# A two-layer encoder trunk on one core: the query norm's VectorE chain queued behind the query transposes, and a reordered opening

## The chip, the core and the metric

The kernel runs on one core of a Trainium2 chip. The metric is the device time of one execution in microseconds (us). A profile records one execution: when each instruction ran on TensorE (PE, its weight loads PEld), VectorE (DVE), ScalarE (ACT), GpSimd (POOL) and on SyncE's queue (SP), and what released it when it had waited.

## The reference

An encoder of two layers on one sequence of 512 tokens, 1024 wide, in float32. What matters here is the first feed-forward block and the query path of the attention branch:

```python
def rms_norm(x, g):
    y = x * rsqrt(mean(x * x, axis=-1) + EPS)
    return y * g
def swiglu(h, w_in, w_out):
    a, b = split(h @ w_in, 2)
    return (silu(a) * b) @ w_out
for l in range(2):
    x = x + 0.5 * swiglu(rms_norm(x, ffn1_norm[l]), ffn1_w_in[l], ffn1_w_out[l])
    h = rms_norm(x, mix_norm[l])
    q, k, v, gu, gv, lx, ly, g = split(h @ w_mix_in[l])
    q = apply_axial_rope(rms_norm(q.reshape(b, s, 8, 64), q_norm[l]), tabs)
    k = apply_axial_rope(rms_norm(k.reshape(b, s, 2, 64), k_norm[l]), tabs)
    ...   # attention, gated MLP, bidirectional LRU; gated sum; output projection
    ...   # cross-attention into 256 memory tokens; a second swiglu block
return rms_norm(x, final_norm)
```

## The kernel before

Activations lie transposed: feature tiles of 128 on the partitions, the 512 tokens along the free dimension. `x` holds 8 such tiles (`KD` = 8). Every float32 operand of a large product is split into a high part (`whi`, `xh`: a cast on ScalarE) and a low part (`wlo`, `xl`: a subtraction on VectorE), and `mm3` issues three matmuls for each product: high by high, high by low, low by high (lines 357 to 359 of the profile).

Weights stream in one order fixed by `plan()`. `Stream.load` starts the DMA of a chunk into one of two `stage` buffers from SyncE's queue. `Stream.split` makes high and low part of a *part* (half a chunk, 1024 columns) in one of four `whi`/`wlo` buffers, up to three parts ahead of the matmuls that take it. The first chunk comes in four smaller parts (256, 256, 512 and 1024 columns), so that the first product can begin early.

A *unit* (`pair_unit`) is 48 matmuls of 512 columns into two PSUM banks; `wide_unit` does 96 into four. All PSUM tiles rotate through one pool of eight banks, so a unit waits until the tile eight places earlier has been read.

**The opening.** `Norm.parts(m)` makes `xh` and `xl` of tile m. `Norm.square(m)` squares the tile on ScalarE and adds it to `nacc` on GpSimd (line 429). After the first unit `norm.finish()` splits `nacc`, sums it over the partitions with two matmuls against `ones_r` (line 395, in `row_scale`), and makes the row `s_row` (lines 400 to 403), by which each unit's result is scaled (lines 533 to 536). SyncE issues the DMAs for `x`, for the small parameters `par` and for the weights in turn, one every 0.47 us.

**The mixer.** While TensorE works through the input projection, side tasks (`attention`, `lru`, `gmlp`: Python generators in `tasks`) are advanced by `tick()`, so their instructions are laid in between. A scheduler then orders each engine's queue by dependences and priorities; each engine works its queue strictly in that order. In `attention`, the query's head norm is `head_squares` (ScalarE squares, line 743, and VectorE reductions `cqq`, line 744), and `head_scale` (a chain of 14 small VectorE operations of 128x32 with the Newton steps of `rsqrt_small`, lines 754 to 760, and one more at line 822 which makes `cq8`). `cq8` is first read by the scores of the attention heads, which come only after the `gu` unit. The rotated queries are transposed on TensorE (line 807, four token tiles t = 0 to 3, a PSUM bank each), copied out on ScalarE (line 813) and split on VectorE (line 816). In the same stretch run a step of the LRU (lines 633 to 663: sigmoid, exponential, tanh, square root on ScalarE; scans on VectorE; its block-diagonal weights split at line 486) and the units `ly` (two, with gelu at line 959) and `gv` (a `wide_unit`).

**Names.** `lam_prep` is a chain of tiny VectorE operations (`lz`) on LRU parameters, once a layer.

Of the kernel before, what the change touches and what calls it, by code (L numbers as in the profile page):

```python
# [14 lines left out]
P = 128  # L15
# [4 lines left out]
L = 2  # L20
# [236 lines left out]
def emit(tc, wts, par, rows, ws_t, bd, xt, memt, const, out):  # L257
# [16 lines left out]
    eps_t = keep.tile([P, 1], F32, name="eps_t")  # L274
    warm = keep.tile([P, 1], F32, name="warm")
    mem_row = keep.tile([P, MEM], F32, name="mem_row")
    pr = [keep.tile([P, NPC], F32, name=f"par{l}") for l in range(L)]
    lam_c = [keep.tile([P, 8], F32, name=f"lam{l}") for l in range(L)]
    keep.tile([P, PAD], F32, name="pad")
    x = keep.tile([P, KD, S], F32, name="x")  # L280
# [5 lines left out]
    def getr(n):  # L286
        return arena.get(n, F32R)
# [77 lines left out]
    def tick(n=1):  # L365
        for _ in range(n):
            for t in list(tasks):
                try:
                    next(t)
                except StopIteration:  # L370
                    tasks.remove(t)
# [35 lines left out]
    class Norm:  # L407


        def __init__(self, gain):  # L410
            self.gain = gain

        def tile(self, m):
            self.parts(m)
# [7 lines left out]
        def square(self, m):  # L422
            if m == 0:
                self.acc = row_p.tile([P, 512], F32, tag="nacc", name="nacc")
                act.activation(self.acc, x[:, m], AF.Square)
                return
            sq = get(1)
            act.activation(sq.f, x[:, m], AF.Square)  # L428
            pool.tensor_tensor(self.acc, self.acc, sq.f, op=ALU.add)  # L429
            sq.free()  # L430

        def sums(self):
# [50 lines left out]

    def split_to(hi, lo, src):
        act.copy(hi, src)  # L485
        dve.tensor_tensor(lo, src, hi.bitcast(F32), op=ALU.subtract)  # L486

    def pair_unit(tag, l, c, bh, bl, n=512, mid=0):
        ps = [bank(), bank()]
        k = 0  # L490
        while k < KD:
            if k == KD // 2:
                tick(mid)
            hi, lo = ws.take((tag, l, c))
            hi = hi.rearrange("p (k t c) -> p k t c", t=2, c=P)
            lo = lo.rearrange("p (k t c) -> p k t c", t=2, c=P)
            for i in range(hi.shape[1]):
                for t in range(2):
                    mm3(ps[t][:, 0:n], hi[:, i, t], lo[:, i, t], bh[k], bl[k], k == 0, k == KD - 1)
                k += 1  # L500
        return ps
# [19 lines left out]


    def ffn(l, w_in, w_out, norm, nxt):
        s_row = None
        for b in range(NB):
            gs = []
            for j in range(b * JB, (b + 1) * JB):
                psa, psb = pair_unit(w_in, l, j, xhk, xlk)
                if s_row is None:
                    s_row = norm.finish()  # L530
                t = get(1)
                g = getr(2)
                dve.tensor_tensor(t.f, psa, s_row, op=ALU.mult)  # L533
                mark["silu"] = act.activation(t.f, t.f, AF.Silu).ins  # L534
                pool.tensor_tensor(t.f, t.f, s_row, op=ALU.mult)  # L535
                dve.tensor_tensor(t.f, t.f, psb, op=ALU.mult)  # L536
                split_to(g.r[:, 0:512], g.r[:, 512:1024], t.f)
                t.free()
                gs.append(g)
                tick()  # L540
            for m in range(KD):
                if b == NB - 1 and m == KD - 1 and isinstance(nxt, FinalNorm):
                    parts = [ws.take((w_out, l, b, m)) for _ in range(2)]
                    for h in range(2):
                        cs = slice(h * 256, h * 256 + 256)
                        ps = bank()[:, 0:256]
                        for k in range(JB):
                            hi, lo = parts[k // 6]
                            c = slice(k % 6 * P, (k % 6 + 1) * P)
                            mm3(ps, hi[:, c], lo[:, c], gs[k].r[:, 0:512][:, cs], gs[k].r[:, 512:1024][:, cs],  # L550
                                k == 0, k == JB - 1)
                        dve.scalar_tensor_tensor(x[:, m, cs], ps, 0.5, x[:, m, cs], op0=ALU.mult, op1=ALU.add)
                        nxt.half(h)
                    continue
                ps = bank()
                for h, (k0, k1) in enumerate(((0, 6), (6, 11))):
                    hi, lo = ws.take((w_out, l, b, m))
                    for k in range(k0, k1):
                        c = slice((k - k0) * P, (k - k0 + 1) * P)
                        mm3(ps, hi[:, c], lo[:, c], gs[k].r[:, 0:512], gs[k].r[:, 512:1024],  # L560
                            k == 0, k == JB - 1)
                dve.scalar_tensor_tensor(x[:, m], ps, 0.5, x[:, m], op0=ALU.mult, op1=ALU.add)
                if b == NB - 1:
                    nxt.tile(m)
                tick()
            for g in gs:
                g.free()


    def mixer(l, norm, nxt):  # L570
# [192 lines left out]
        def attention():  # L763
# [39 lines left out]
            for t in range(NTT):  # L803
                ps = bank()
                for pr_ in range(4):
                    c0 = t * 512 + pr_ * P
                    pe.transpose(ps[:, pr_ * P:(pr_ + 1) * P], qrot.f[:, c0:c0 + P], ident)
                p3 = ps.rearrange("p (a b) -> p a b", a=4)
                parts = []
                for e in range(2):  # L810
                    q4 = qt[e].r.rearrange("p (a b) -> p a b", a=4)[:, :, t * P:(t + 1) * P]
                    own = slice(e * 64, e * 64 + 64)
                    act.copy(q4[own], p3[own])
                    parts.append((q4, own, slice(64 - e * 64, 128 - e * 64)))
                for q4, own, oth in parts:
                    dve.tensor_tensor(q4[oth], p3[own], q4[own].bitcast(F32), op=ALU.subtract)
                if t == 1:
                    yield
            qrot.free()
            cq = head_scale(qss, 8, "cq")  # L820
            cq8 = small.tile([P, 8, NTT], F32, tag="cq8", name="cq8")
            dve.tensor_scalar(cq8, cq, HD ** -0.5, None, op0=ALU.mult)
            yield
# [422 lines left out]
    def lam_prep(l):  # L1246

        lam = pr[l][:, PC["lam"]:PC["lam"] + 8]
        z = [small.tile([P, 8], F32, tag=f"lz{i}", name=f"lz{i}") for i in range(5)]
        dve.tensor_scalar(z[0], lam, -1.0, None, op0=ALU.mult)  # L1250
        dve.tensor_tensor(z[1], lam, z[0], op=ALU.min)
        with tc.issue_after(mark["silu"]):
            act.activation(z[1], z[1], AF.Exp)
# [13 lines left out]
        return pr[l][:, PC[nm]:PC[nm] + 8]  # L1267

    def load_x(j):
        m0, m1 = ((0, 1), (1, 2), (2, 4), (4, 8))[j]  # L1270
        sp.dma_start(out=x[:, m0:m1], in_=xt[:, m0:m1])
        if j == 0:
            sp.dma_start(out=pr[0], in_=par[:, 0])

    pool.memset(ones, 1.0)
    pool.memset(eps_t, EPS)
    dve.tensor_copy(ones_r, ones)
    ws.load([(0, 256), (256, 512), (512, 1024), (1024, 2048)], load_x)
    nrm = Norm(gains(0, "ffn1"))
    ps = bank()  # L1280
    for _ in range(9):
        pe.matmul(ps[:, 0:P], lhsT=ones, rhs=ones, start=True, stop=True)
# [2 lines left out]
        for m in ms:  # L1285
            nrm.parts(m)
    ws.load()
    sp.dma_start(out=pr[1], in_=par[:, 1])
    sp.dma_start(out=cst, in_=const)
    for m in range(KD):  # L1290
        nrm.square(m)
# [31 lines left out]
```

## Time and profile before

| | us |
|---|---|
| median of three runs (2667.14 to 2667.82) | 2667.79 |
| the profiled execution, by the clock of the runs | 2665.21 |
| its span in the trace | 2663.4 |
| TensorE busy in the span | 2626.9 (99%) |
| VectorE, ScalarE, GpSimd busy | 1391.7, 1163.3, 399.4 |

The profiled execution lies 2.6 us below the median of the runs. A matmul's busy time overlaps the next one's: 512 columns show 0.39 us each, but follow one another every 0.227 us at the full clock. "Granted clock" is the share of TensorE's full clock (2.4 GHz) that the chip allowed; 0.50 is 1.2 GHz. What matters is where TensorE stood idle, and which engine's result ended each wait.

### The profile page before, as it was taken

How to read it: one execution, taken by the hardware profiler on the slowest of the kernel's cores; microseconds unless marked ns; L12 is line 12 of the kernel's file. 1: busy time of each engine (PE TensorE's matmuls, PEld its weight loads, DVE VectorE, ACT ScalarE, POOL GpSimd, SP SyncE). 2: the span in 40 equal slices, each digit the busy share in tenths (PEclk: the TensorE clock that was granted, in tenths of full speed). 3: DMA queues.
4: the chain of work that ended last, by engine and by line, in shares of the span. 5: the costliest groups of instructions: out<-in, count | busy, mean ns of one | idle time of the engine just before them, and what ended most of it. 6: DMA issues, size and time to landing. Idle time of an engine off the chain costs nothing.

```text
span 2663.4 us, 30204 instructions
## 1 busy us (share of the span) xinstructions
PE 2626.9 (99%) x12213; PEld 2187.6 (82%) x12213; DVE 1391.7 (52%) x1965; ACT 1163.3 (44%) x1656; POOL 399.4 (15%) x301
## 2 busy tenths in 40 slices
PE   9999999999999999999999999999999999999998
PEld 7888888788878888888888888878888888888886
DVE  6434457766655554334443344587675664643343
ACT  5322337966634443222332223488575343422223
POOL 3101115100021021001111011240000300210111
PEclk9999999999999999999999999999999999999999
DMA  5232232222223222232322322322222232322222
GB/s 181 80 118 103 77 115 72 87 72 71 95 103 112 91 99 103 80 111 87 111 95 84 128 95 76 120 77 71 72 80 98 93 127 80 111 86 97 109 77 75
DMA packets 50123, 254.31 MB, mean 95 GB/s; under 512 B 5440, under 2 KB 11072, under 8 KB 31808
## 3 DMA queue, kind: packets, MB, share of 16 engines
q1 hardware_dynamic: 49984, 252.39, 27.0%
q8 instruction: 95, 1.56, 0.2%
q14 instruction: 44, 0.36, 0.0%
HBM read 250.27 MB, written 2.10 MB: 95 GB/s over the span
## 4 chain that ended last, share of the span: by engine, by line
PE 91%; DVE 4%; ACT 3%; POOL 1%; issue 1%; DMA 0%; SPq 0%; DVEq 0%; POOLq 0%; ACTq 0%
PE ps L357 29%; PE ps L359 29%; PE ps L358 29%; PE ps L870 1%; PE ps L841 1%; PE ps L858 1%; POOL slot L1023 1%; DVE wlo L339 1%; DVE slot L486 1%; ACT whi L338 0%; DVE slot L1019 0%; ACT slot L485 0%; DMA x<-in_xt 0%; DVE rsy L387 0%; POOL nacc L429 0%
## 5 line engine op out<-in xcount | busy, mean ns | idle before, releaser
L338 ACT CAST whi<-stage 128x1024 fp32r<-128x1024 f32 (+2 forms) x506 | 491.6, 973 | 1034.5 <-PE ps L358 905.1
L339 DVE TENSOR_TENSOR wlo<-stage,whi 128x1024 fp32r<-128x1024 f32 (+2 forms) x506 | 589.0, 1165 | 465.2 <-ACT whi L338 463.4
L357 PE MATMUL ps<-xh,whi 128*128 128x512 f32 x2048 | 802.2, 392 | 0.6 <-ACT xh L419 0.5
L358 PE MATMUL ps<-xl,whi 128*128 128x512 f32 x2048 | 798.7, 390 | 2.1 <-DVE xl L420 2.1
L359 PE MATMUL ps<-xh,wlo 128*128 128x512 f32 x2048 | 798.1, 390 | 0.0
L357 PE MATMUL ps<-slot,whi 128*128 128x512 f32 (+1 forms) x1291 | 488.0, 378 | 2.6 <-ACT slot L485 2.6
L358 PE MATMUL ps<-slot,whi 128*128 128x512 f32 (+1 forms) x1291 | 486.8, 377 | 1.1 <-DVE slot L486 1.1
L359 PE MATMUL ps<-slot,wlo 128*128 128x512 f32 (+1 forms) x1291 | 486.4, 377 | 0.0
L358 PEld LDWEIGHTS ps<-xl,whi 128*128 128x128 f32 x2048 | 385.1, 188 | 83.7 <-DVE xl L420 3.9
L357 PEld LDWEIGHTS ps<-xh,whi 128*128 128x128 f32 x2048 | 385.0, 188 | 81.7 <-ACT xh L419 2.2
L359 PEld LDWEIGHTS ps<-xh,wlo 128*128 128x128 f32 x2048 | 384.9, 188 | 79.9
L535 POOL TENSOR_TENSOR slot<-slot,srow 128x512 f32<-128x512 f32 x88 | 148.8, 1691 | 900.3 <-ACT slot L534 900.3
L357 PEld LDWEIGHTS ps<-slot,whi 128*128 128x128 f32 x1291 | 242.9, 188 | 48.3 <-ACT slot L485 3.4
L358 PEld LDWEIGHTS ps<-slot,whi 128*128 128x128 f32 x1291 | 242.9, 188 | 46.7 <-DVE slot L486 1.9
L359 PEld LDWEIGHTS ps<-slot,wlo 128*128 128x128 f32 x1291 | 242.9, 188 | 44.6
L485 ACT CAST slot<-slot 128x512 fp32r<-128x512 f32 (+2 forms) x149 | 89.5, 608 | 281.3 <-DVE slot L536 216.1
L429 POOL TENSOR_TENSOR nacc<-nacc,slot 128x512 f32<-128x512 f32 x62 | 97.0, 1565 | 568.3 <-ACT slot L428 298.9
L533 DVE TENSOR_TENSOR slot<-ps,srow 128x512 f32<-128x512 f32 x88 | 60.8, 691 | 216.1 <-PE ps L359 216.0
L486 DVE TENSOR_TENSOR slot<-slot,slot 128x512 fp32r<-128x512 f32 (+2 forms) x149 | 103.6, 703 | 91.0 <-ACT slot L485 90.8
L536 DVE TENSOR_TENSOR slot<-slot,ps 128x512 f32<-128x512 f32 x88 | 60.5, 688 | 111.9 <-POOL slot L535 111.9
L486 DVE TENSOR_TENSOR slot<-ps,slot 128x512 fp32r<-128x512 f32 (+1 forms) x144 | 92.5, 655 | 39.6 <-ACT slot L485 38.5
L485 ACT CAST slot<-ps 128x512 fp32r<-128x512 f32 (+1 forms) x144 | 77.2, 563 | 57.6 <-PE ps L359 54.3
(192 smaller groups left out, 2270.4 us busy)
## 6 DMA issues: line engine op xcount, KB each, us to landing
stage<-in_wts SPq DMA_DIRECT2D x141, 1024.0 KB, 4.8
stage<-in_wts SPq DMA_DIRECT2D x64, 704.0 KB, 4.0
stage<-in_wts SPq DMA_DIRECT2D x77, 512.0 KB, 3.3
stage<-in_wts SPq DMA_DIRECT2D x8, 768.0 KB, 4.3
slot<-in_memt SPq DMA_DIRECT2D x6, 512.0 KB, 3.2
slot<-in_bd SPq DMA_DIRECT2D x4, 512.0 KB, 5.9
out<-slot SPq DMA_DIRECT2D x8, 256.0 KB, 2.5
x<-in_xt SPq DMA_DIRECT2D x1, 1024.0 KB, 9.1
```

Source lines behind the costliest of these rows:

```text
L338: act.copy(hi[:, 0:n], t)
L339: dve.tensor_tensor(lo[:, 0:n], t, hi[:, 0:n].bitcast(F32), op=ALU.subtract)
L357: pe.matmul(ps, lhsT=ah, rhs=bh, start=start, stop=False)
L358: pe.matmul(ps, lhsT=ah, rhs=bl, start=False, stop=False)
L359: pe.matmul(ps, lhsT=al, rhs=bh, start=False, stop=stop)
L429: pool.tensor_tensor(self.acc, self.acc, sq.f, op=ALU.add)
L485: act.copy(hi, src)
L486: dve.tensor_tensor(lo, src, hi.bitcast(F32), op=ALU.subtract)
L533: dve.tensor_tensor(t.f, psa, s_row, op=ALU.mult)
L535: pool.tensor_tensor(t.f, t.f, s_row, op=ALU.mult)
L536: dve.tensor_tensor(t.f, t.f, psb, op=ALU.mult)
L841: pe.matmul(ps, lhsT=qt[e].r[:, c0:c0 + P], rhs=kk.r[:, k0:k0 + 512], start=part == 0, stop=part == 1)
```

## The change

Three edits. First, in `attention`, the query's `head_scale` chain is tied on VectorE behind the last split of the query transposes (`tc.issue_after(last)`: an order on the same engine's queue, no semaphore), and in `lam_prep` the first operation is tied behind the last feed-forward split. Second, in the opening, `par` (both layers in one transfer) and the tiles 1 and 2 to 3 of `x` are started from ScalarE's queue, tiles 0 and 4 to 7 from SyncE's, the latter ahead of the first chunk's last part; the squares of the first norm are added on VectorE. Third, in the first feed-forward block `norm.finish()` is called in the middle of the second unit instead of after the first, and the first two units are scaled together after it.

```diff
     class Norm:
-        def __init__(self, gain):
+        def __init__(self, gain, adder=pool):
             self.gain = gain
+            self.adder = adder
...
-            pool.tensor_tensor(self.acc, self.acc, sq.f, op=ALU.add)
+            self.adder.tensor_tensor(self.acc, self.acc, sq.f, op=ALU.add)
...
-    def pair_unit(tag, l, c, bh, bl, n=512, mid=0):
+    def pair_unit(tag, l, c, bh, bl, n=512, mid=0, hook=None):
...
             if k == KD // 2:
                 tick(mid)
+                if hook is not None:
+                    hook()
...
-                psa, psb = pair_unit(w_in, l, j, xhk, xlk)
-                if s_row is None:
-                    s_row = norm.finish()
...
+                held.append(pair_unit(w_in, l, j, xhk, xlk, hook=finish if norm is first and j == 1 else None))
+                if norm is first and j == 0:
+                    continue
+                if not row:
+                    finish()
+                s_row = row[0]
+                for psa, psb in held:
...
             qrot.free()
-            cq = head_scale(qss, 8, "cq")
+            with tc.issue_after(last):
+                cq = head_scale(qss, 8, "cq")
...
-        dve.tensor_scalar(z[0], lam, -1.0, None, op0=ALU.mult)
+        with tc.issue_after(mark["lo"]):
+            dve.tensor_scalar(z[0], lam, -1.0, None, op0=ALU.mult)
...
     def load_x(j):
-        m0, m1 = ((0, 1), (1, 2), (2, 4), (4, 8))[j]
-        sp.dma_start(out=x[:, m0:m1], in_=xt[:, m0:m1])
-        if j == 0:
-            sp.dma_start(out=pr[0], in_=par[:, 0])
-
+        if j in (0, 2):
+            m0, m1 = ((0, 1), None, (4, 8))[j]
+            sp.dma_start(out=x[:, m0:m1], in_=xt[:, m0:m1])
+
+    act.dma_start(out=prm, in_=par)
+    for m0, m1 in ((1, 2), (2, 4)):
+        act.dma_start(out=x[:, m0:m1], in_=xt[:, m0:m1])
+    pool.memset(eps_t, EPS)
     pool.memset(ones, 1.0)
-    pool.memset(eps_t, EPS)
+    act.activation(warm, eps_t, AF.Square)
...
-    nrm = Norm(gains(0, "ffn1"))
+    first = nrm = Norm(gains(0, "ffn1"), dve)
...
-    sp.dma_start(out=pr[1], in_=par[:, 1])
```

The lines of the changed file are about 13 higher than before (816 becomes 829, 486 becomes 488). In the mixer only VectorE's queue differs. In layer 0, before, the chain (`cqc` and `cq` are its last two operations) stands ahead of the split of the LRU weights and of the key splits (794, 795):

```order
L386 SCALAR_TENSOR_TENSOR rsa<-rsa,cqv 128x32
L387 SCALAR_TENSOR_TENSOR rsy<-rsa,rsy 128x32
L760 TENSOR_TENSOR cqc<-rsy,scol 128x32
L822 TENSOR_SCALAR cq_3252<-cqc 128x32
L486 TENSOR_TENSOR slot_655<-slot_249,slot_2757 128x1024
L794 TENSOR_TENSOR slot_1628<-ps,slot_1628 64x512
L795 TENSOR_TENSOR slot_1628<-ps,slot_1628 64x512
```

In the changed kernel, the same place on VectorE and, further on, the place to which the chain went, behind the second four query splits (829) of layer 0:

```order
L757 TENSOR_REDUCE cqq<-slot_2607 128x8
L488 TENSOR_TENSOR slot_654<-slot_308,slot_2756 128x1024
L807 TENSOR_TENSOR slot_1627<-ps,slot_1627 64x512
L808 TENSOR_TENSOR slot_1627<-ps,slot_1627 64x512
```

```order
L829 TENSOR_TENSOR slot_1893<-ps,slot_1893 64x4x128
L829 TENSOR_TENSOR slot_1760<-ps,slot_1760 64x4x128
L829 TENSOR_TENSOR slot_1893<-ps,slot_1893 64x4x128
L766 TENSOR_TENSOR cqs_3230<-scol 128x4
L767 TENSOR_TENSOR cqq<-cqq,cqs_3230 128x32
L770 TENSOR_SCALAR cqv<-cqq 128x32
```

The chain is now interleaved with the next LRU step and followed by the low parts of the next weights; layer 1 is changed alike. In the opening, ScalarE's queue before, from the high part of the first chunk's third part on:

```order
L338 CAST whi<-stage 128x512
L428 ACTIVATE slot_150<-x 128x512
L419 ACTIVATE xh<-x,par_79 128x512 x2
L428 ACTIVATE slot_150<-x 128x512
L338 CAST whi<-stage 128x1024
L428 ACTIVATE slot_150<-x 128x512
L419 ACTIVATE xh<-x,par_79 128x512 x4
L428 ACTIVATE slot_150<-x 128x512
L428 ACTIVATE slot_159<-x 128x512 x3
L338 CAST whi<-stage 128x1024 x3
L485 CAST slot_231<-nacc 128x512
```

And in the changed kernel:

```order
L339 CAST whi<-stage 128x512
L421 ACTIVATE xh<-x,par 128x512 x4
L339 CAST whi<-stage 128x1024
L421 ACTIVATE xh<-x,par 128x512 x2
L427 ACTIVATE nacc<-x 128x512
L430 ACTIVATE slot_149<-x 128x512 x4
L430 ACTIVATE slot_158<-x 128x512 x3
L339 CAST whi<-stage 128x1024 x4
L487 CAST slot_260<-nacc 128x512
```

The squares (430) now stand together between the last `xh` and the high parts of the second unit, and `nacc`'s cast (487) behind four high parts instead of three. On TensorE the two row-sum matmuls (396) stand in the changed kernel behind the first 24 matmuls of the second unit.

## Rows read from the trace of the kernel before

**Rows 1.** Page, part 1: busy time, share of the span, instructions of each engine.

```profile
PE 2626.9 (99%) x12213; PEld 2187.6 (82%) x12213; DVE 1391.7 (52%) x1965; ACT 1163.3 (44%) x1656; POOL 399.4 (15%) x301
```

**Rows 2.** PE's waits over the span: us in total, times, longest.

```profile
PE ps L807 <- DVE slot L816: 8.7, 4, 4.8
PE ps L357 <- ACT slot L633: 4.1, 2, 2.0
```

**Rows 3.** Timeline, layer 0, VectorE: start, duration, operation, out<-in, shapes, count.

```profile
439.85 0.56 DVE L754 TENSOR_TENSOR cqq<-cqq,cqs 128x32 f32<-128x32 f32 x1
...
451.32 1.20 DVE L822 TENSOR_SCALAR cq<-cqc 128x32 f32<-128x32 f32 x1
452.44 1.21 DVE L486 TENSOR_TENSOR slot<-slot,slot 128x1024 fp32r<-128x1024 f32 x1
```

**Rows 4.** Timeline, layer 0: what follows, with idle time and its releaser in brackets.

```profile
453.68 1.34 ACT L648 ACTIVATE slot<-slot,lam 128x512 f32<-128x512 f32 x2 [6.31 <-DVE slot L486]
...
467.26 1.09 PE L807 MATMUL ps<-cst,slot 128*128 128x128 f32 x4 [4.77 <-DVE slot L816]
...
471.80 0.76 PE L357 MATMUL ps<-whi,xh 128*128 128x512 f32 x1 [2.03 <-ACT slot L633]
```

**Rows 5.** Timeline, layer 1: the same places.

```profile
1774.31 0.63 ACT L658 ACTIVATE slot<-slot 128x512 f32<-128x512 f32 x1 [5.63 <-DVE slot L651]
...
1782.96 1.08 PE L807 MATMUL ps<-cst,slot 128*128 128x128 f32 x4 [3.27 <-DVE slot L816]
...
1787.49 0.76 PE L357 MATMUL ps<-whi,xh 128*128 128x512 f32 x1 [2.03 <-ACT slot L633]
```

**Rows 6.** Timeline, opening.

```profile
13.65 2.56 ACT L419 ACTIVATE xh<-x,par 128x512 fp32r<-128x512 f32 x4 [0.62 <-DMA x<-in_xt]
...
16.12 2.18 ACT L428 ACTIVATE slot<-x 128x512 f32<-128x512 f32 x4
...
23.80 0.62 ACT L485 CAST slot<-nacc 128x512 fp32r<-128x512 f32 x1 [2.23 <-POOL nacc L429]
...
24.47 0.79 PE L395 MATMUL ps<-slot,ones_r 128*128 128x512 f32 x1 [2.58 <-ACT slot L485]
```

**Rows 7.** Windows: busy us (instructions) by engine, granted clock, DMA share, GB/s.

```profile
24.47:27.60 3.13, 3.13 (x7) 2.48 (x8) 3.13 (x4) 2.81 (x4) 1.11 (x1) 0.50 0.51 136
471.80:474.50 2.70, 2.70 (x7) 2.12 (x8) 2.70 (x4) 2.67 (x4) 0.00 (x0) 0.50 0.80 337
1787.49:1792.32 4.83, 4.83 (x11) 3.77 (x12) 4.17 (x6) 4.79 (x6) 0.37 (x1) 0.50 0.73 244
```

**Rows 8.** Timeline, PE: last matmul of the second unit, and the next one.

```profile
37.20 0.39 PE L359 MATMUL ps<-xh,wlo 128*128 128x512 f32 x1
37.43 0.39 PE L357 MATMUL ps<-xh,whi 128*128 128x512 f32 x1
```

**Rows 9.** Windows, behind the second four query splits of layer 0: columns as in rows 7.

```profile
482.00:492.65 10.65, 10.65 (x49) 8.82 (x48) 7.62 (x10) 10.59 (x15) 0.00 (x1) 1.00 0.16 52
```

**Rows 10.** Timeline: a small VectorE operation with no GpSimd work beside it.

```profile
499.61 0.16 DVE L387 SCALAR_TENSOR_TENSOR rsy<-rsa,rsy 128x4 f32<-128x4 f32 x1
```

**Rows 11.** One line's instructions in the opening: count, duration ns min/median/max.

```profile
L420 DVE SCALAR_TENSOR_TENSOR xl<-x,par,xh x8: 740/1012/1815, 5.3 to 18.6; 128x512 fp32r<-128x512 f32 x8
```

**Rows 12.** Windows, opening: columns as in rows 7.

```profile
1.50:12.20 10.70, 9.26 (x34) 6.71 (x33) 5.04 (x10) 6.61 (x12) 1.79 (x2) 1.00 0.89 307
```

**Rows 13.** Timeline, SyncE's queue: the issue of tiles 4 to 7 of `x`.

```profile
4.50 0.43 SPq L1271 DMA_DIRECT2D x<-in_xt  x1
```

**Rows 14.** Page, part 5: groups of instructions, busy us and mean ns of one.

```profile
L338 ACT CAST whi<-stage 128x1024 fp32r<-128x1024 f32 (+2 forms) x506 | 491.6, 973 | 1034.5 <-PE ps L358 905.1
L339 DVE TENSOR_TENSOR wlo<-stage,whi 128x1024 fp32r<-128x1024 f32 (+2 forms) x506 | 589.0, 1165 | 465.2 <-ACT whi L338 463.4
L536 DVE TENSOR_TENSOR slot<-slot,ps 128x512 f32<-128x512 f32 x88 | 60.5, 688 | 111.9 <-POOL slot L535 111.9
```

More of the change, by code (lines that the diff above doesn't have):

```diff
@@ L276, in emit @@
     mem_row = keep.tile([P, MEM], F32, name="mem_row")
-    pr = [keep.tile([P, NPC], F32, name=f"par{l}") for l in range(L)]
+    prm = keep.tile([P, L, NPC], F32, name="par")
+    pr = [prm[:, l] for l in range(L)]
     lam_c = [keep.tile([P, 8], F32, name=f"lam{l}") for l in range(L)]
@@ L485, in split_to @@
         act.copy(hi, src)
-        dve.tensor_tensor(lo, src, hi.bitcast(F32), op=ALU.subtract)
-    def pair_unit(tag, l, c, bh, bl, n=512, mid=0):
+        return dve.tensor_tensor(lo, src, hi.bitcast(F32), op=ALU.subtract).ins
+    def pair_unit(tag, l, c, bh, bl, n=512, mid=0, hook=None):
         ps = [bank(), bank()]
@@ L523, in ffn, with finish @@
     def ffn(l, w_in, w_out, norm, nxt):
-        s_row = None
+        row, held = [], []
+        def finish():
+            row.append(norm.finish())
         for b in range(NB):
@@ L527, in ffn @@
             for j in range(b * JB, (b + 1) * JB):
-                psa, psb = pair_unit(w_in, l, j, xhk, xlk)
-                if s_row is None:
-                    s_row = norm.finish()
[L531 to L540, printed above, removed]
+                held.append(pair_unit(w_in, l, j, xhk, xlk, hook=finish if norm is first and j == 1 else None))
[5 more added lines that the diff above has]
+                for psa, psb in held:
+                    t = get(1)
+                    g = getr(2)
+                    dve.tensor_tensor(t.f, psa, s_row, op=ALU.mult)
+                    mark["silu"] = act.activation(t.f, t.f, AF.Silu).ins
+                    pool.tensor_tensor(t.f, t.f, s_row, op=ALU.mult)
+                    dve.tensor_tensor(t.f, t.f, psb, op=ALU.mult)
+                    mark["lo"] = split_to(g.r[:, 0:512], g.r[:, 512:1024], t.f)
+                    t.free()
+                    gs.append(g)
+                    tick()
+                held = []
             for m in range(KD):
@@ L815, in attention @@
                 for q4, own, oth in parts:
-                    dve.tensor_tensor(q4[oth], p3[own], q4[own].bitcast(F32), op=ALU.subtract)
+                    last = dve.tensor_tensor(q4[oth], p3[own], q4[own].bitcast(F32), op=ALU.subtract).ins
                 if t == 1:
```

## The prediction, made before the changed kernel ran

> **What bounds the kernel now.** First the page's busy times: TensorE (PE) is busy 2626.9 of 2663.4 us [rows 1], so no engine can be relieved in general; all that can be won is the 36.5 us in which PE stands idle, and the matmuls that run at the lower clock behind such idle times. Next PE's waits, sorted by what ended them: the largest single one is line 807, the transposes of the rotated queries, waiting for VectorE's line 816: 8.7 us in four waits, one of 4.8; behind it 4.1 us in two waits of the projection for ScalarE's sigmoid, line 633 [rows 2]. Then the timeline backwards from those waits.
>
> Layer 0: PE waits 4.77 us ahead of the transposes at 467.26 and 2.03 ahead of the `gv` unit at 471.80 [rows 4]. Transposes of t = 2 need a bank that the splits of t = 0 (line 816) must leave; those stand behind the LRU's step on both engines. ScalarE started that step (line 648) at 453.68, after 6.31 us idle, released by VectorE's line 486 [rows 4]. And VectorE reached 486 only at 452.44, because from 439.85 it worked through 15 operations of 128x32, the query norm chain, up to `cq` [rows 3]. So the stretch from 453.68 to 471.80 hangs on that chain. Layer 1 has the same picture with another entry: ScalarE's line 658 idles 5.63 us for VectorE's 651, then PE waits 3.27 and 2.03 us [rows 5].
>
> The opening: PE's first unit ends at 24.47 - 2.58 = 21.89; the row-sum matmuls wait until 24.47 for ScalarE's cast of `nacc`, which waited 2.23 us for GpSimd's last addition [rows 6]. Behind that idle time the granted clock is 0.50 (1.2 GHz) until 27.60 [rows 7]. The second unit ends at 37.43, where the next unit's first matmul stands [rows 8]. The gap between two matmuls at full clock is 37.43 - 37.20 = 0.23.
>
> **The change part by part.** *The chain moved, layer 0.* It costs VectorE from 439.85 to 452.44 = 12.6 us, 0.84 an operation [rows 3]. Without it 486 can run as soon as ScalarE's half of that split is there, and ScalarE's line 648 when its 6.31 us of idle time begin, at 447.37; everything that hung on it comes 6.31 earlier. PE's idle time in the stretch is 4.77 + 2.03 = 6.8 and a few tenths between the two groups of transposes, more than 6.31, so PE can take the whole shift: **6.3 us**. Up to 0.8 us of wait remains, plus what the transposes gain when they run at full clock (2.2 us together at 1.09 each now, after a long idle time), so about 2. Behind the wait, seven matmuls stand in the 2.70 us from 471.80, the seventh beginning at its end, at a granted clock of 0.50 [rows 7]: six at 0.227 would take 1.36, so 1.3 is lost. A wait of about 2 may or may not bring the low clock again; I take half back, **0.7** (ends 0 and 1.3).
>
> *Layer 1.* By the same reading 5.63 us of ScalarE's idle time go; PE has 3.27 + 2.03 and the same few tenths: **5.6 us**. There eleven matmuls begin in 4.83 us at 0.50 [rows 7], against 11 x 0.227 = 2.5: 2.3 lost, of which I take half, **1.2** (ends 0 and 2.3).
>
> *The chain's new place.* It now runs on VectorE behind the second four query splits, ahead of the next LRU step. What an operation costs there no row shows. Bounds: 0.16 (a small operation with no GpSimd work beside it [rows 10]) and 1.20 (the last one of the chain now, [rows 3]). In that stretch GpSimd does nothing and VectorE is busy 7.62 of 10.65 us [rows 9], so 3.0 are free; the present chain runs beside GpSimd's rope products, and in the opening `xl` takes 740 to 1815 ns for one shape while GpSimd adds [rows 11]. I take 0.2: 15 x 0.2 = 3.0, covered by VectorE's 3.0 free us: **0**. What would be late if that cover is gone: line 651 of the next LRU step, for which ScalarE waits, and ScalarE, busy 10.59 of 10.65 [rows 9], casts all weights for PE. `cq8` itself is read only by the scores, after the `gu` unit.
>
> *Opening, transfers.* The DMA engines are busy 0.89 at 307 GB/s from 1.5 to 12.2 us [rows 12]: the transfers are limited by bytes, not by issue. Tiles 4 to 7 of `x` land at 13.65 [rows 6]. The change puts them ahead of the first chunk's last part. Then 3.25 MB (`x` 2.1, the first chunk 1.05, `par` 0.1) have to come before both are there: 1.5 + 3.25/0.307 = 12.1, call it 12.3. ScalarE casts two tiles (2.56/4 = 0.64 each [rows 6]), then the weights' last part (0.97, low part 1.17 [rows 14]), so PE has its last operands at about 15.9 and, with 22 of the 24 matmuls on that part left, ends the first unit at 20.9 instead of 21.9.
>
> *Opening, squares and row scale.* ScalarE then has two more `xh`, seven squares (2.18/4 = 0.55 each [rows 6]) and the second unit's first high part: 15.95 + 4.4 + 1.0 = 21.4; VectorE, with seven additions of 0.69 [rows 14], brings the low part at 22.75. The second unit's first 24 matmuls end at 27.3, the row sums follow at 27.75 (a wait of 0.2, since the cast of `nacc` stands behind a fourth high part), and the other 24 end at 33.4. Against 37.43 that is 4.0. It takes for granted that PE's stop between 12.5 and 15.9, for the operands, does not lower the clock; if it does, it costs about what it did at 24.47: seven matmuls began in 3.13 us [rows 7], 3.13 - 7 x 0.227 = 1.5. Then 2.6. I take **3.3**. Bounds: 0 (transfers no earlier, ScalarE's squares ahead of the second unit cost what the row scale gave) and about 7 (no idle time at all between the two units, 37.43 - 21.89 - 50 x 0.227 = 4.2; and tiles 4 to 7 earlier not only by bytes, 1.0, but also by four issues of SyncE fewer ahead of them, 1.9).
>
> *At nothing:* the tie of `lam_prep`, off every wait of PE, and three DMA issues of 0.43 us [rows 13] on ScalarE before any data has landed. Two more held banks of eight are free again some 8 us before their turn by the same working.
>
> *Sum:* 3.3 + 6.3 + 0.7 + 5.6 + 1.2 = 17.1. The profiled execution of before took 2665.2 by the runs' clock, so 2648.1; the median of the runs lies 2.6 above it: **2650.7**.
>
> *A rule against the transfers.* The row says that the engines are at 0.89 and 307 GB/s [rows 12] while SyncE issues from one queue; tiles 4 to 7 were issued at 4.50 [rows 13], and four issues less ahead of them, one every 0.47, make that 2.6. The Trainium skill, "DMA: Bandwidth & Descriptors", section "Issuing engines are not separate DMA queues", says that transfers begun by several engines end on the same 16 DMA engines and that a second issuer saves only the sequencer's time. The row agrees as far as it goes, since the engines are nearly full with one issuer. By the rule the transfers' share of the opening would be nothing, about 1.0 of the 3.3, and the sum 16.1; by my reading the order of the bytes still brings that 1.0.
>
> **The rivals.** *A. The opening gives nothing* (chance 0.20): the transfers share full engines [rows 12], so that what is put ahead in the order comes no sooner, while the weights' last part comes later; PE then stops at about 12.5 for 3 us or more, at half the clock behind it (1.5), and the second unit waits for ScalarE's squares. That eats the 2.58 + 1.5 won at 24.47. Time: 2650.7 + 3.3 = 2654.0. The rule of the Trainium skill named above leads part of this way. Against it: half a megabyte is really moved behind `x`.
>
> *B. The mixer gives half* (0.10): another wait takes the place of the one removed, above all ScalarE's sigmoid 633 [rows 2], which also waits for products that PE ends late, or the copies of the transposes. Half of 13.8 is 6.9: 2657.6.
>
> *C. The change does not do it in the mixer* (0.08): VectorE's chain covered a wait that ScalarE has anyway (a table load, the loads of LRU weights), so 648 starts when it did; only the opening counts: 2664.5, no change. Against it: ScalarE's wait names 486, and 486 follows the chain without a gap [rows 3, 4].
>
> *D. The opening gives 7* (0.04): 2647.
>
> *E. Slower* (0.05): the chain costs 1.20 an operation in its new place too. 15 x 1.20 = 18 against 3.0 free us: 15 us late at line 651, and since ScalarE there has nothing to spare [rows 9] the weights' casts and PE come as much later, in both layers: +30 against -17.1, that is 2667.8 + 12.9 = 2680.7. It decides from where two chains cost more than they win and 0.2% besides: 15p - 3.0 = (17.1 + 5.3)/2, so p = 0.95 an operation. Against it: GpSimd stands still there, and up to three parts of weights lie ready.
>
> **How the numbers follow.** The forecast has 0.53; its own range is 2647.5 to 2653 (the clock's halves 1.9 either way, the opening 1.3 to 4.0 with 1 us for the runs). To hold 8 in 10 the range must reach A, B and D: 2646 to 2660, 0.87. 0.2%, 5.3 us, is about what a measurement of this kernel can tell from no change. Faster by more than that: forecast, A, B and D, 0.87; within it C, 0.08; slower E, 0.05.
>
> **What the profile of the changed kernel would show.** Right: PE's waits list line 807 with next to nothing; ScalarE's 648 in layer 0 and 658 in layer 1 start with no idle time for VectorE; the `gv` unit begins 6 us earlier against the LRU's matmuls ahead of it; the chain's operations at about 0.2 us, some ten microseconds later; in the opening no wait at the row sums over 0.5 us and the second unit's end near 33.4. Wrong: chain operations near 1 us; a new PE wait, longer than 3, for 633 or for `xl` and `wlo`; tiles 4 to 7 landing after 13; a half clock at 15 to 19 us; a stop of PE at the start of the second unit longer than 1 us.

## The result and the profile after

The changed kernel takes 2650.93 us (median of 4 runs, 2649.55 to 2651.13) against 2667.47 for the kernel before beside it (4 runs, 2666.27 to 2667.82): a ratio of 0.9938, 95% interval 0.9923 to 0.9952, 16.5 us faster. The forecast was 2650.7. The profiled execution of the changed kernel took 2650.86 with a span of 2648.9, so between the two profiled executions there are 14.35 us, where the sum of the prediction said 17.1. The forecast hit because a second estimate was off the other way; the section on the prediction shows how.

PE's waits in the changed kernel (us in total, times, longest), the same view as [rows 2]:

```profile
PE ps L358 <- DVE slot L972: 5.0, 2, 2.5
...
PE ps L396 <- DVE slot L488: 1.6, 4, 0.6
...
PE ps L820 <- DVE slot L829: 0.8, 1, 0.8
```

The wait of the transposes (line 807, now 820) fell from 8.7 to 0.8, the row sums of the opening (396) wait 0.6. In place of the 4.1 us for the sigmoid there are now 5.0, two of 2.5, for line 972: the scaling of the second `ly` unit on VectorE, which holds the bank that `gv` wants.

Layer 0 in the timeline of the changed kernel:

```profile
443.07 1.35 ACT L661 ACTIVATE slot<-slot,lam 128x512 f32<-128x512 f32 x2
...
443.66 1.24 DVE L340 TENSOR_TENSOR wlo<-stage,whi 128x1024 fp32r<-128x1024 f32 x1
...
443.78 2.28 POOL L740 TENSOR_TENSOR slot<-slot,slot 128x512 f32<-128x512 f32 x1
...
449.64 2.54 POOL L658 TENSOR_TENSOR slot<-slot,slot 128x512 f32<-128x512 f32 x2
...
450.96 1.77 DVE L672 TENSOR_TENSOR slot<-slot,slot 128x512 f32<-128x512 f32 x1 [2.43 <-POOL slot L658]
...
456.46 2.81 DVE L829 TENSOR_TENSOR slot<-ps,slot 64x512 fp32r<-64x512 f32 x4
...
459.42 0.63 PE L820 MATMUL ps<-cst,slot 128*128 128x128 f32 x4 [0.79 <-DVE slot L829]
...
462.53 0.64 PE L358 MATMUL ps<-whi,xh 128*128 128x512 f32 x1 [2.48 <-DVE slot L972]
```

All times here are 4.33 us earlier than before because of the opening. ScalarE's LRU step (648, now 661) starts at 443.07 instead of 453.68 [rows 4]: 10.61, of which 10.61 - 4.33 = 6.28 are the chain's, as predicted (6.3), and its idle time is gone. But the `gv` unit starts at 462.53 instead of 471.80 [rows 4]: 9.27 - 4.33 = 4.9. The 1.4 us between the two were lost at line 672, where VectorE waits 2.43 us for GpSimd. In layer 1 ScalarE's step (658, now 671) starts at 1759.51 instead of 1774.31, which less the lead of 9.09 that the kernel has by then is 5.7, as predicted (5.6); but line 672 waits 1.85 us, and `gv` starts at 1773.98 instead of 1787.49 [rows 5]. Behind layer 0's half clock the changed kernel is 9.09 us ahead, so layer 1 wins 13.51 - 9.09 = 4.4 here instead of 5.6.

The clock behind the wait, windows as in [rows 7]:

```profile
462.53:466.25 3.72, 3.72 (x10) 2.94 (x11) 3.72 (x6) 3.68 (x5) 0.00 (x0) 0.54 0.65 251
1773.98:1776.98 3.00, 3.00 (x8) 2.37 (x8) 3.00 (x5) 2.97 (x4) 0.00 (x0) 0.53 0.74 311
```

The half clock came back in both layers: nine matmuls in layer 0 (six to seven before), seven in layer 1 (eleven before).

The chain in its new place, timeline of VectorE (first operations and the last):

```profile
473.15 0.19 DVE L767 TENSOR_TENSOR cqq<-cqq,cqs 128x32 f32<-128x32 f32 x1
473.38 0.18 DVE L770 TENSOR_SCALAR cqv<-cqq 128x32 f32<-128x32 f32 x1
...
477.25 0.17 DVE L836 TENSOR_SCALAR cq<-cqc 128x32 f32<-128x32 f32 x1
```

15 operations of 0.17 to 0.19, as predicted (0.2), where they took 0.84 beside GpSimd's rope products [rows 3].

The opening, timeline of the changed kernel:

```profile
5.94 0.72 ACT L421 ACTIVATE xh<-x,par 128x512 fp32r<-128x512 f32 x1 [1.67 <-DMA x<-in_xt]
...
6.71 0.73 PE L358 MATMUL ps<-xh,whi 128*128 128x512 f32 x2 [1.48 <-ACT xh L421]
...
10.96 1.34 ACT L421 ACTIVATE xh<-x,par 128x512 fp32r<-128x512 f32 x2 [0.65 <-DMA x<-in_xt]
...
14.56 0.50 PE L360 MATMUL ps<-xh,wlo 128*128 128x512 f32 x1 [0.53 <-DVE wlo L340]
...
14.91 3.75 ACT L430 ACTIVATE slot<-x 128x512 f32<-128x512 f32 x7
...
21.47 0.69 DVE L431 TENSOR_TENSOR nacc<-nacc,slot 128x512 f32<-128x512 f32 x1
...
21.61 0.74 PE L360 MATMUL ps<-xh,wlo 128*128 128x512 f32 x2 [0.76 <-DVE wlo L340]
...
27.30 0.50 PE L396 MATMUL ps<-slot,ones_r 128*128 128x512 f32 x1 [0.58 <-DVE slot L488]
...
33.10 0.39 PE L358 MATMUL ps<-xh,whi 128*128 128x512 f32 x1
```

The second unit's end moved from 37.43 [rows 8] to 33.10, 4.33 us. Tiles 4 to 7 of `x` are there at 10.96 instead of 13.65 [rows 6]. But the first tile comes later: ScalarE waits 1.67 us for it, and PE begins the first unit at 6.71, where the kernel before began at 5.30:

```profile
5.30 1.22 PE L357 MATMUL ps<-xh,whi 128*128 128x512 f32 x2
```

After that PE stops for operands 0.53 and 0.76 us only, and the granted clock stays at 1.00.

### The profile page after: what moved, and what is told of

Its sections match the earlier page's. It is cut to its first block, busy times and chain, and to the rows that moved or that the text cites. A ratio compares the mean times of both kernels' runs of the same rounds, so it can differ in the third digit from the quotient of the medians.

```text
span 2648.9 us, 30205 instructions
## 1 busy us (share of the span) xinstructions
PE 2621.2 (99%) x12213; PEld 2184.9 (82%) x12213; DVE 1374.3 (52%) x1972; ACT 1163.3 (44%) x1657; POOL 391.5 (15%) x294
## 4 chain that ended last, share of the span: by engine, by line
PE 91%; DVE 3%; POOL 3%; ACT 1%; issue 1%; DMA 0%; DVEq 0%; SPq 0%; POOLq 0%; ACTq 0%
PE ps L358 29%; PE ps L360 29%; PE ps L359 29%; PE ps L884 1%; PE ps L855 1%; PE ps L872 1%; DVE wlo L340 1%; POOL slot L1037 1%; DVE slot L488 1%; POOL slot L740 1%; POOL slot L745 0%; POOL slot L747 0%; DVE slot L1033 0%; DMA x<-in_xt 0%; ACT slot L487 0%
## 5 line engine op out<-in xcount | busy, mean ns | idle before, releaser
L431 POOL TENSOR_TENSOR nacc<-nacc,slot 128x512 f32<-128x512 f32 x55 | 85.2, 1548 | 557.3 <-ACT slot L430 288.2
```

Of the source, the lines that this page charges most:

```text
L431: self.adder.tensor_tensor(self.acc, self.acc, sq.f, op=ALU.add)
```

## The experiments

Each run stands beside runs of the kernel before; that kernel's runs lay between 2661.5 and 2669.8 us over all of them, and its medians beside the different runs between 2665.6 and 2667.5. A difference of less than 2 us between two runs that did not stand side by side therefore rests on their traces and not on the times. The changed kernel is 2650.9.

**The tie alone and the opening alone.** Kernel before plus the tie of the query chain:

```diff
-            cq = head_scale(qss, 8, "cq")
+            with tc.issue_after(last):
+                cq = head_scale(qss, 8, "cq")
```

> The kernel before with the query chain's tie alone. Theory (the tie frees ScalarE's LRU step as predicted, but GpSimd's LRU product comes late and cuts the shift from 6.3 to 4.9): the gains of the changed kernel's trace, 4.6 in layer 0 and 5.4 in layer 1, 10.0 us below before. By the prediction's own terms 13.8. Rival (the mixer's gain came from elsewhere in the change): under 2 us.

And the changed kernel without it:

> The changed kernel with the query chain back in its old place: the opening (and the tie of lam_prep) alone. Theory (the second unit ends 4.3 us earlier and nothing later gives it back): 4.4 us below before. The prediction's term was 3.3, its rival A 0.

Measured: the tie alone 2656.45 (before 2666.64; ratio 0.9964, 0.9951 to 0.9977), 10.2 us faster, which is what the trace of the changed kernel gives for the two layers (4.8 and 5.4, with the half clock). The opening alone 2660.61 (0.9978, 0.9969 to 0.9988), 6.0 faster by the runs; in its trace the second unit ends at 33.01, 4.4 earlier than in the one of before. The two sum to 16.2 of the 16.5. Part of the 1.6 by which the opening's 6.0 exceeds 4.4 lies in the kernel before: in the trace of the tie alone, whose opening is the old one, the row sums wait longer and the second unit ends at 38.37, not 37.43.

```profile
25.31 0.80 PE L395 MATMUL ps<-slot,ones_r 128*128 128x512 f32 x1 [3.95 <-ACT slot L485]
```

So the old opening differs by 1 us between executions, and the profile of before showed one of its better ones. The new opening's second unit ends at 33.0 to 33.2 in all seven traces that have it unaltered. The rest of the 1.6 is open. The tie of `lam_prep` is part of the opening in this run and was not run by itself.

**Which part of the opening.** Transfers in the order of the changed kernel, but on one queue (`x` ahead of the chunk's last part, all from SyncE), and in the old order on one queue:

```diff
-    act.dma_start(out=prm, in_=par)
-    for m0, m1 in ((1, 2), (2, 4)):
-        act.dma_start(out=x[:, m0:m1], in_=xt[:, m0:m1])
```

> The changed kernel with all transfers of the opening on SyncE's queue, x still ahead of the first chunk's last part. Theory (the order of the bytes on full DMA engines decides, not the queue): tiles 4 to 7 are there within 0.5 us of 10.96 and the second unit ends within 0.5 us of 33.1; time that of the changed kernel. Rival (the second queue's earlier issue is what brought x sooner; they are issued at about 4.0 here, not 2.6): 1 to 2 us later, 1 to 2 us above the changed kernel.

> The changed kernel with the transfers of x and par in the old order and all on SyncE's queue (tiles 4 to 7 again behind the first chunk's last part; par of both layers in one transfer). Theory (the row scale in the second unit carries the opening's gain, since a later x only eats into time that the squares and the second unit's weights need anyway): second unit ends within 0.7 us of 33.1, time within 1 us of the changed kernel. Rival (the transfers' order is worth the 1.0 of the prediction, or the 2.2 by which the first unit ended earlier): 1.0 to 2.2 us above.

Measured: 2652.0 (2650.25 to 2653.73) on one queue in the new order, and 2650.87 (2650.67 to 2651.63) in the old order, which has the second unit end at 32.63. Tiles 4 to 7 came 1.6 us later on one queue (12.52), as the rival said and against what I had expected, yet the second unit ended at 32.84. Neither the queue nor the order is worth anything here. The second unit starts at 19.69 in the changed kernel, 20.69 in the old order and 21.43 in the new order on one queue, and ends within 0.5 us all the same: an earlier `x` ends the first unit earlier, and then the second waits for ScalarE's squares and VectorE's low part (the 0.76 us at 21.61). The rule of the Trainium skill that the prediction weighed ("DMA: Bandwidth & Descriptors", section "Issuing engines are not separate DMA queues") held for the time: the second queue's share of the gain is nothing. For the bytes it did not hold here: from 6.5 to 13 us the DMA engines moved 430 GB/s in the changed kernel (427 to 432 in all nine traces with two queues), against 384 with the new order on one queue (379 to 391 in all five traces with one).

Row scale after the first unit again, and additions on GpSimd again:

```diff
-hook=finish if norm is first and j == 1 else None
+hook=None
...
-                if norm is first and j == 0:
-                    continue
```

> The changed kernel with the row scale made after the first unit again. Theory: PE waits for the squares and the sum (about 2 to 3 us from the first unit's end at 19.7) and the clock is 0.50 behind it: 3 to 4.5 us above the changed kernel. Rival (earlier x and VectorE's additions make the sum early enough): under 1 us above.

```diff
-    first = nrm = Norm(gains(0, "ffn1"), dve)
+    first = nrm = Norm(gains(0, "ffn1"))
```

> The changed kernel with the squares added on GpSimd again. Theory: seven additions of 1.3 to 1.5 us end about 25 to 26 instead of 22.1, the row sums come about as they do now or up to 1.5 us later inside the second unit: 0 to 1.5 us above. Rival (GpSimd beside VectorE's low parts stretches both, as xl before, 740 to 1815 ns): 2 to 4 us above.

Measured: 2653.59 (2653.35 to 2656.33) without the deferral, 2.7 above the changed kernel; 2654.62 (2653.75 to 2656.12) with the additions on GpSimd, 3.7 above, where I had expected 0 to 1.5 and the rival said 2 to 4. PE's wait at the row sums in the one and in the other:

```profile
23.04 0.50 PE L396 MATMUL ps<-slot,ones_r 128*128 128x512 f32 x1 [3.16 <-ACT slot L487]
```

```profile
15.55 13.04 POOL L431 TENSOR_TENSOR nacc<-nacc,slot 128x512 f32<-128x512 f32 x7 [14.59 <-ACT slot L430]
...
29.30 1.52 PE L396 MATMUL ps<-slot,ones_r 128*128 128x512 f32 x2 [3.61 <-ACT slot L487]
```

Seven additions take GpSimd 13.04 us (1.86 each; VectorE needs 0.78 each), so the sum is late even for the middle of the second unit. The second unit ends at 37.4 to 38.5 with neither edit (three traces, with the old transfers), 35.6 with the additions alone, 38.1 with the deferral alone, and 33.1 with both. The additions are worth some 2 to 3 us alone, the deferral 2.5 on top of them, and nothing that shows without them.

**What holds the mixer at 4.9 and 4.4.** The products of the second LRU step on VectorE:

```diff
-                    pool.tensor_tensor(xi.f, xi.f, xc.f, op=ALU.mult)
+                    (dve if c == 1 else pool).tensor_tensor(xi.f, xi.f, xc.f, op=ALU.mult)
```

> The changed kernel with the two LRU products of the second step (line 658) on VectorE instead of behind the rope products on GpSimd. Theory (GpSimd, late by 2.4 us at line 672, holds the query splits): that wait goes, two operations of 0.69 are added ahead, the splits come about 1.4 us earlier, PE's wait of 2.48 shrinks as much, 1.4 to 2.5 us a layer, 3 to 5 us below the changed kernel. Rival (VectorE is full there, or PE's wait for line 972 hangs on ScalarE's table loads): 0 to 1 us, or slower.

Measured: 2647.83 (2645.95 to 2649.32; ratio 0.9930, 0.9913 to 0.9947), every run below those of the changed kernel, 3.1 us below its median (2.3 when each is taken against the kernel before beside it; the intervals of the two ratios overlap, so the traces must decide). Layer 0 in its timeline, and the clock behind the wait:

```profile
449.26 1.78 DVE L672 TENSOR_TENSOR slot<-slot,slot 128x512 f32<-128x512 f32 x1
...
455.08 2.82 DVE L829 TENSOR_TENSOR slot<-ps,slot 64x512 fp32r<-64x512 f32 x4
...
461.16 0.47 PE L358 MATMUL ps<-whi,xh 128*128 128x512 f32 x1 [2.05 <-ACT slot L646]
```

```profile
461.16:463.40 2.24, 2.24 (x10) 1.88 (x11) 2.24 (x4) 2.22 (x3) 0.00 (x0) 1.00 0.92 388
1770.25:1772.50 2.25, 2.25 (x10) 1.88 (x11) 2.25 (x4) 2.22 (x3) 0.00 (x0) 1.00 0.98 411
```

VectorE no longer idles at 672, the query splits come 1.38 earlier, and so does `gv`; what is left is a wait of 2.05 for the sigmoid, about the rest of 2 that the prediction had left. Against the kernel before, and less the lead that the kernel has ahead of the layer, `gv` now starts 6.4 us earlier in layer 0 and 5.7 in layer 1, where the prediction said 6.3 and 5.6. So GpSimd's lateness is what held back the shift. The clock stays at 1.00 behind the waits of 2.05 and 1.24, and with it the two layers win 7.3 and 7.5 us, where the prediction had 7.0 and 6.8. That the shorter wait is why the clock stayed up is not shown (see the half clock below).

**The chain's price in the new place.** 30 more operations of 128x32 behind it, on a scratch tile:

```diff
                 cq = head_scale(qss, 8, "cq")
+                for i in range(30):
+                    dve.tensor_scalar(dum, dum, 1.0, None, op0=ALU.mult)
```

> The changed kernel with 30 more small VectorE operations (128x32, on a scratch tile) behind the query chain in its new place, about 6 us more. Theory (the 3.0 free us there are the cover, and ScalarE has none to spare): the chain's excess goes to ScalarE's line 671 and on to PE, 3 to 6 us a layer, 6 to 12 us above the changed kernel. Rival (parts split ahead cover it): under 2 us.

```profile
L838 DVE TENSOR_SCALAR dum<-dum x60: 154/175/1155, 473.2 to 1799.6; 128x32 f32<-128x32 f32 x60
```

Measured: 2651.54 (2651.14 to 2652.2), 0.6 above, within the spread. I had expected 6 to 12. The scheduler laid the added operations between those of the chain and between larger ones, where they overlap: in the 16 us behind the query splits VectorE is busy 15.48 us instead of 12.21, so the added load is 3.3 us a layer and not 6. The next LRU step's operations on VectorE came up to 2.2 us late by it (676 at 484.42 instead of 482.04), but ScalarE's queue kept its times and VectorE's next split for PE (488) starts at 489.05 instead of 488.90. The chain has room for 3.3 us more than it takes; where the room ends was not tried.

**Another place for the chain.** Kernel before, tied behind the key splits (794, 795), hence behind the LRU weights' split but beside the rope products:

```diff
-                        dve.tensor_tensor(l0[other], ps[rs_], h0[rs_].bitcast(F32), op=ALU.subtract)
+                        last = dve.tensor_tensor(l0[other], ps[rs_], h0[rs_].bitcast(F32), op=ALU.subtract).ins
...
+            with tc.issue_after(last):
+                cq = head_scale(qss, 8, "cq")
```

> The kernel before with the query chain tied behind the key splits (794, 795) instead of the query splits: it no longer stands ahead of the LRU weights' split, but still runs beside GpSimd's rope products. Theory (what counts is that the chain runs where GpSimd stands still, so that it takes 3 us and not 12): ScalarE's LRU step starts 6.3 us earlier in layer 0, but then VectorE's line 651 comes late by most of the 12.6 us of the chain; gain under 3 us. Rival (the order alone counts, any place behind line 486 will do): as the tie alone, 10 us below before.

```profile
448.42 1.34 ACT L648 ACTIVATE slot<-slot,lam 128x512 f32<-128x512 f32 x2
...
454.28 1.22 DVE L385 TENSOR_TENSOR rsa<-rsy 128x32 f32<-128x32 f32 x1
...
456.26 0.63 ACT L960 ACTIVATE slot<-slot 128x512 f32<-128x512 f32 x1 [2.93 <-DVE slot L959]
...
466.08 1.09 PE L807 MATMUL ps<-cst,slot 128*128 128x128 f32 x4 [2.55 <-DVE slot L816]
```

Measured: 2664.16 against 2665.83 (ratio 0.9997, 0.9988 to 1.0006): no gain that can be told from none. ScalarE's step starts early, but five of the first six operations still cost 0.65 to 1.26 each, and line 959 and the query splits come late instead. The operations behind 458.4, when GpSimd is through, cost 0.18 to 0.19 here too. Passing the LRU weights' split is not enough; the place has to be one where the chain is short.

**Two tries at a better kernel.** Both on top of the kernel with the products on VectorE. The side tasks advanced in the middle of the second `ly` unit, and then the LRU's alone:

```diff
-            ps = pair_unit("ly", l, c, xhk, xlk)
+            ps = pair_unit("ly", l, c, xhk, xlk, mid=c)
```

> A version to beat both: the changed kernel with the two LRU products on VectorE (as in e8) and the side tasks advanced in the middle of the second ly unit, so that the LRU's matmuls and the last query transposes stand ahead of its second 24 matmuls. Theory (PE's remaining waits of 2.05 and 1.24 ahead of gv are for ScalarE's sigmoid, which then has 24 matmuls, 5.4 us, more time): these waits go, 3 to 4 us below e8, about 2644. Rival (the later steps of the side tasks then meet a full ScalarE, and the splits of weights come late): 0 to 5 us above e8.

```diff
-            ps = pair_unit("ly", l, c, xhk, xlk)
+            ps = pair_unit("ly", l, c, xhk, xlk, hook=(lambda: next(lru_task)) if c == 1 else None)
```

> As e8, and only the LRU's side task advanced in the middle of the second ly unit; the last query transposes stay behind that unit. Theory (the transposes, which e13 moved ahead too, then found no free bank; the sigmoid alone profits from the 24 matmuls between): no wait ahead of gv, none at line 820, 2 to 3.5 us below e8's 2647.8, about 2645. Rival (the reordered ScalarE queue costs elsewhere as much): equal to e8 or slower.

Measured: 2651.8 (2651.6 to 2656.12) and 2649.35 (2649.1 to 2650.82), where I had expected about 2644 and 2645. Neither is below 2647.83; the second is too near to it to be called slower. In the first the transposes moved too and wait for a bank; in the second both waits are gone and `gv` starts at 458.71, but ScalarE's queue came out in another order, the casts of the next weights behind it:

```profile
456.53 0.63 PE L820 MATMUL ps<-cst,slot 128*128 128x128 f32 x4 [3.43 <-DVE slot L829]
```

```profile
474.94 2.94 ACT L339 CAST whi<-stage 128x1024 fp32r<-128x1024 f32 x3
...
476.04 0.50 PE L358 MATMUL ps<-whi,xh 128*128 128x512 f32 x1 [0.76 <-ACT whi L339]
478.03 0.79 PE L359 MATMUL ps<-wlo,xh 128*128 128x512 f32 x1 [1.48 <-DVE wlo L340]
...
476.00:481.50 5.50, 3.97 (x10) 2.93 (x11) 5.49 (x11) 5.45 (x7) 0.00 (x0) 0.69 0.43 140
```

The wait moved into the `gv` unit, with the half clock behind it. The kernel with the products on VectorE keeps the lowest median of all.

**The clock behind the wait.** The changed kernel with more work for PE in it:

```diff
+                for _ in range(9 if t == 3 else 1):
-                for pr_ in range(4):
+                    for pr_ in range(4):
```

> The changed kernel with the transposes of the last token tile repeated eight times more (32 transposes of 128 columns into the same bank, the same result), so that PE works through most of the 2.48 us wait ahead of gv. Theory (the half clock behind that wait, 9 matmuls in layer 0 and 7 in layer 1 at 0.43 instead of 0.23 apart, follows from the idle time): no stretch at 0.50 there, 2 to 3 us below the changed kernel. Rival (the clock falls anyway, or small transposes do not hold it): within 1 us, or slower by what the extra transposes take.

```profile
462.00:465.00 3.00, 3.00 (x22) 2.69 (x21) 3.00 (x5) 2.56 (x4) 0.00 (x0) 1.00 0.73 306
465.00:468.00 3.00, 3.00 (x15) 2.49 (x14) 1.65 (x3) 2.99 (x5) 1.06 (x1) 1.00 0.66 224
```

In the place itself the theory holds: no half clock in layer 0, `gv` starts 0.7 us later (463.24) and its later matmuls are 0.9 us ahead. But the time is 2658.15 (2656.51 to 2659.91), 7 us above, where I had expected 2 to 3 below: the scheduler ordered later parts of the mixer otherwise, and PE there waits 4.1 us for line 991, for which the changed kernel does not wait. So for the time this run is inconclusive, and one place without a half clock is little (see the half clock below).

## Why the prediction came out right, and where it was wrong

**The tie, mechanism.** Right. ScalarE's LRU step moved by 6.28 us, the transposes' wait went, the chain costs 0.19 an operation where GpSimd stands still, and nothing behind it comes late.

**The tie, size.** The step "PE can take the whole shift" overrated both layers: 4.9 and 4.4 us came of 6.3 and 5.6. It looked at PE's idle time and not at every engine that feeds the shifted stretch. VectorE's line 672 (before: 659) needs GpSimd's LRU product too. Before, GpSimd was through with its two products at 454.8 and VectorE came for the first at 460.05, so no wait in the trace named it:

```profile
451.20 3.60 POOL L645 TENSOR_TENSOR slot<-slot,slot 128x512 f32<-128x512 f32 x2
...
460.05 0.69 DVE L659 TENSOR_TENSOR slot<-slot,slot 128x512 f32<-128x512 f32 x1
```

Now it is the last, and not only because VectorE comes earlier: in layer 0 GpSimd's rope products of the last two token tiles take 5.0 and 5.9 us instead of 4.0 and 4.1. Without these 2.8 us its first LRU product would have been ready at about 448.1 (an estimate: 449.64 - 2.8 + 1.27), and VectorE is free for it at 448.5, so it would not have waited. The kernel before, beside the chain, and two tiles earlier beside a split of weights:

```profile
437.71 1.51 DVE L339 TENSOR_TENSOR wlo<-stage,whi 128x1024 fp32r<-128x1024 f32 x1 [0.73 <-ACT whi L338]
...
438.10 2.27 POOL L727 TENSOR_TENSOR slot<-slot,slot 128x512 f32<-128x512 f32 x1
...
447.14 1.28 POOL L727 TENSOR_TENSOR slot<-slot,slot 128x512 f32<-128x512 f32 x1
```

The product takes 1.28 beside the chain and 2.27 when a large split started just before it; with the chain gone, the last two tiles of layer 0 meet such a split (443.66 and 443.78 above: 1.12 us of the split are left, and the product takes 1.0 longer). In layer 1 of the changed kernel the product starts first, and it is the split that takes longer (2.29 instead of 1.24):

```profile
1755.12 1.29 POOL L740 TENSOR_TENSOR slot<-slot,slot 128x512 f32<-128x512 f32 x1
...
1755.20 2.29 DVE L340 TENSOR_TENSOR wlo<-stage,whi 128x1024 fp32r<-128x1024 f32 x1 [0.18 <-ACT whi L339]
```

The Trainium skill, "SBUF — State Buffer", section "Who interferes with whom", says that VectorE and GpSimd share one pair of ports under a lock, for a VectorE instruction with two SBUF inputs (as these splits have) against a GpSimd instruction that reads SBUF: who starts first holds it, the other stands still. Durations and order in these rows agree with that. That the LRU product caps the shift is shown by the run with the products on VectorE; that the lock is what lengthened the rope products rests on these rows and was not isolated.

**The half clock.** Half of each dip (the time lost at half clock) was counted back, 1.9 in all. In layer 0 it came back longer (0.2 lost, nine matmuls), in layer 1 shorter (0.9 won). Halving was a guess between two ends, and neither layer lay in the middle. The other traces show how wide it is. The wait of 2.48 stands ahead of `gv` in both layers of seven of them (the changed kernel, the tie alone, both transfer runs, no deferral, additions on GpSimd, the longer chain). In 13 of these 14 places the clock fell to half, and the 26th matmul of `gv` came 1.4 to 2.7 us later than 25 steps of 0.227; in one it stayed up, and the 26th came 0.5 late. That place is layer 0 of the new order on one queue:

```profile
462.25:465.25 3.00, 3.00 (x13) 2.48 (x14) 3.00 (x5) 2.97 (x4) 0.00 (x0) 1.00 0.69 287
```

In the run with the products on VectorE, with waits of 2.05 and 1.24, the clock did not fall at all. So the same wait does not always bring the same loss, and the size of this term was luck in either direction.

**The opening.** 4.33 instead of 3.3. The prediction's working gave 4.0 without a half clock and 2.6 with one; the clock did not fall, so it is the first that came, but not by the steps that led to it. The transfers' 1.0 is nothing (two runs). The stop of PE from 12.5 to 15.9 shrank to 0.53 us ahead of 14.56, from both sides: PE came to it later, having started 1.4 us later, and the operands were there earlier, tiles 4 to 7 at 10.96 where the sum let ScalarE begin at 12.3 (the DMA engines moved 430 GB/s from 6.5 to 13 us, 384 before, where the sum used 307 for the whole time from 1.5 on). Nor did it hang on the earlier tiles: in the old order on one queue they came at 14.01, PE stopped 0.88 us, and the clock stayed at 1.00 as well. What gained is the row scale in the second unit, together with VectorE's additions; the prediction named both, and treated the additions as a cost (4.9 us of VectorE) rather than as what makes the deferral work.

**From the profile to the median.** The three terms came to 4.33 + 4.8 + 5.4 = 14.5 (with the half clock; the spans differ by 14.5) instead of 17.1. The prediction then added 2.6, the distance of before's profiled execution from its median, to the new time; the changed kernel's profiled execution lies on its median. About 1 us of that distance can have belonged to the old opening, which varies from one execution to the next (second unit's end 37.43, 38.37, 38.46) and is now gone; the rest is open, though the half clock in the mixer also differs between executions (the opening alone, whose mixer is the old one, lost 1.0 us more there than the profile of before). The two errors, 2.7 in the sum and 2.6 in what was added, cancel; the agreement within 0.3 us is luck. Each alone would have left the time inside the range given.

**The rivals.** B, another wait in the place of the one removed, came partly: 4.9 + 4.4 of 11.9, and the wait was for GpSimd, which it did not name. A, C, D and E did not come: the opening gave more than its term and less than 7, ScalarE did start when predicted, and the chain costs 0.19 an operation, with 3.3 us of added load behind it costing nothing measurable.

## What to carry to other kernels

When a stalled stretch is moved forward, list for each of its instructions all engines that feed it, with the time at which each input was ready: the input that was ready second can become the new releaser, and no wait in the old profile names it. A chain of small VectorE operations belongs where GpSimd stands still, here 0.19 us an operation instead of 0.84, and moving it changes what GpSimd runs beside. If the profiled execution lies off the median, find which stage varies before carrying the distance over to the new time. A deferral pays only if the work that must be done by the later moment is quick enough: 2.5 us here with the additions on VectorE, nothing that shows with them on GpSimd.

## What was not expected of the hardware

GpSimd's 128x512 product took 1.28 us beside a queue full of 128x32 VectorE operations, and 2.27 beside one 128x1024 split: the small ones slowed themselves (0.17 to 1.3 us) and hardly the other engine. PE kept full clock behind idle times of 2.05 and 1.24 us in one trace, and fell to half behind one of 2.48 in 13 of 14 places in seven others, at times five matmuls after it (the tie alone, layer 0). With two engines issuing, the transfers from 6.5 to 13 us ran at 430 GB/s where one reached 384, and the kernel gained nothing by it.
